# Sums of weight halves formed ahead and kept in DRAM, and an eighth seven-product square in six groups of a transformer block

## The chip, the cores and the metric

One core of one Trainium2 chip runs the whole kernel. The metric is the device time of one execution in microseconds (us). The kernel before took 2002.9 us, the median of three runs (2002.39 to 2003.01). A step called faster or slower here is one of more than 0.2%.

## The reference, cut to what matters

One layer of a block with two kinds of mixing: a chunked mLSTM with eight heads, and a sparse attention with sixteen heads in four groups. The width is 4096, the sequence 256 rows, everything in float32. Almost all of the arithmetic is in three large matrix products; the rest stands between them.

```python
h = _rmsnorm(x, norm_w[layer])
u = h @ w_in[layer]                       # 4096 x 13376: q, k, v and gates of both mixers
...
y_ml = hm.reshape(B, S, ML_WIDTH) * jax.nn.sigmoid(ml_o) * jax.nn.silu(ml_z)
y_ns = _nsa(ns_q, ...) * jax.nn.silu(ns_z)
x = x + jnp.concatenate([y_ml, y_ns], axis=-1) @ w_out[layer]
x = x + jax.nn.sigmoid(x @ ple_gate[layer]) * (p[layer] @ ple_proj[layer])
```

## The kernel before

**Units.** The weights are cut into units of 128 partitions x 1024 floats (512 KB), and the program is written out by hand as one list of them. SP loads a unit into one of six `raw` buffers (L1527 and the lines around it). ScalarE copies it to `whi`, rounded to the short float that TensorE multiplies in one pass (L1543). VectorE forms the rest, `wlo = raw - whi` (L1546). The activations are split the same way into `sh` and `sl`. TensorE adds up three products for each block, whi by sh, whi by sl and wlo by sh. There are four `whi` and four `wlo` buffers, and VectorE's subtraction is issued three units ahead of TensorE's use:

```python
for n in range(N):
    if n + LOOK < N:
        split_low(n + LOOK)        # VectorE, LOOK = 3
    ...
    load_some()                    # SP, while a raw buffer is free
    ...
    un["mm"](*splits.pop(n))       # TensorE
    ...
        split_high(n + 1 + LOOK)   # ScalarE
```

Loads are issued in the order of the units, each as soon as `held_raw` says that a buffer is free. All engines run their own instructions in order, so an instruction of another task that stands between two `wlo` subtractions on VectorE puts off the second of them.

**Stages.** First come the early pair groups and the "wide" groups (`wide_group`, TensorE lines L968 and L970). A wide unit has 12 matmuls. Beside the wide groups run the side tasks: the attention of the four head groups (L530 to L664), the convolutions of the mLSTM's q and k (L694, L696), the mLSTM itself, and the mixed activations (`t_mix`, L840 to L848). The wide groups that matter below are, in order, `nq2`, `nq3`, `mq0`, `mk0`, `mq1`, `mk1`, `mv2`, `mv3`. Then come the late pair groups, numbered -6 to 7 (`pair_group`, L1246): gates, the output projection and the last gate.

**Squares.** A pair group multiplies by 1024 columns at once, two halves whose results stand in the tiles `mm` and `sd`. Its 16 "squares" of 256 rows each are done in one of two ways. A square marked C takes the plain way: eight block products, 24 matmuls, two units. A mixed square takes seven block products in the manner of Strassen and Winograd, 21 matmuls. It has a part a (two units) and, after a C square that stands between, a part c (two units). Part c needs sums of the square's weight halves. VectorE forms them in place, in the two `raw` buffers that the square therefore holds until part c, by four dependent additions of 128 x 512 (L1327, L1329, L1331, L1332 in `sums`). Each follows a `wlo` subtraction of a later unit (`split_and_sum`). For the first unit of part a only one half is split (`split_one`, L1553 and L1556). A plan gives the order of the squares of a group; squares written in brackets share one C square between their parts.

```python
FULL = _plan((0,), (3, 5, 7, (9, 11), 13, 1), (2, 4, 6, 8, 10, 12), (14, 15))
PLANS = {g: FULL for g in (-5, -4, -3, -2, 1, 2)}
```

So each of these six groups has seven mixed squares and nine C squares.

## Time and profile before

| | |
|---|---|
| median of three runs | 2002.9 us |
| span of the profiled execution | 2001.0 us |
| what lies around the span in the median | 1.9 us |
| TensorE matmul (PE) busy | 1992.9 us, 9626 records |
| VectorE (DVE) busy | 1720.8 us |
| ScalarE (ACT) busy | 1210.8 us |
| GpSimd (POOL) busy | 23.3 us |
| DMA, mean over the span | 211 GB/s |

The shares are averages over stages with different limits, and matmuls overlap one another: the mean length of one matmul in the list of groups (379 to 389 ns) is longer than the distance from one to the next, which the chain of waits gives. Stretches of the program are named below by their time from the start of the span: the wide groups run from about 441 to 849 us, four of the six groups (-5 to -2) from about 934 to 1248 us and the other two (1 and 2) from 1415 to 1572 us.

### The profile page before, as it was taken

How to read it: one execution, taken by the hardware profiler on the slowest of the kernel's cores; microseconds unless marked ns; L12 is line 12 of the kernel's file. 1: busy time of each engine (PE TensorE's matmuls, PEld its weight loads, DVE VectorE, ACT ScalarE, POOL GpSimd, SP SyncE). 2: the span in 40 equal slices, each digit the busy share in tenths (PEclk: the TensorE clock that was granted, in tenths of full speed). 3: DMA queues.
4: the chain of work that ended last, by engine and by line, in shares of the span. 5: the costliest groups of instructions: out<-in, count | busy, mean ns of one | idle time of the engine just before them, and what ended most of it. 6: DMA issues, size and time to landing. Idle time of an engine off the chain costs nothing.

```text
span 2001.0 us, 26995 instructions
## 1 busy us (share of the span) xinstructions
PE 1992.9 (100%) x9626; PEld 1736.7 (87%) x9626; DVE 1720.8 (86%) x2235; ACT 1210.8 (61%) x1583; POOL 23.3 (1%) x59
## 2 busy tenths in 40 slices
PE   9999999999999999999999999999999999999998
PEld 8888888888888888888888888888888888888887
DVE  7797779787677776869999999999999998999988
ACT  7655556556666646566565666666555566666655
POOL 0000000000000000000000000000000000000000
PEclk9999999999999999999999999999999999999999
DMA  9656767575445455646666667565767674767664
GB/s 374 236 194 233 259 232 246 165 243 180 166 150 168 151 190 170 204 152 214 214 209 222 211 214 237 190 221 184 247 217 234 231 239 159 237 211 240 203 239 152
DMA packets 119351, 422.08 MB, mean 211 GB/s; under 512 B 14583, under 2 KB 14991, under 8 KB 119216
## 3 DMA queue, kind: packets, MB, share of 16 engines
q1 hardware_dynamic: 116880, 413.90, 61.2%
q0 software_dynamic: 2144, 6.44, 1.3%
q8 instruction: 75, 1.23, 0.2%
q14 instruction: 60, 0.49, 0.1%
q10 hardware_dynamic: 192, 0.02, 0.0%
HBM read 416.08 MB, written 4.23 MB: 210 GB/s over the span
## 4 chain that ended last, share of the span: by engine, by line
PE 98%; DVE 1%; DMA 0%; ACT 0%; issue 0%; SPq 0%; DVEq 0%; ACTq 0%
PE mm L1246 36%; PE sd L1246 34%; PE mm L968 14%; PE mm L970 7%; PE sd L639 1%; PE mm L1080 1%; PE sd L628 1%; PE sd L867 1%; PE sd L275 0%; DMA raw<-in_w_in 0%; PE sd L579 0%; PE sd L595 0%; PE sd L594 0%; PE sd L593 0%; PE mm L1056 0%; PE mm L1057 0%
## 5 line engine op out<-in xcount | busy, mean ns | idle before, releaser
L1543 ACT ACTIVATE whi<-raw 128x1024 fp32r<-128x1024 f32 x852 | 888.7, 1054 | 676.2 <-DVE raw L1332 155.1
L1546 DVE TENSOR_TENSOR wlo<-raw,whi 128x1024 fp32r<-128x1024 f32 x852 | 1035.3, 1221 | 186.4 <-ACT whi L1543 176.6
L1246 PE MATMUL mm<-whi,sh 128*128 128x512 f32 x897 | 281.6, 381 | 0.0
L1246 PE MATMUL mm<-wlo,sh 128*128 128x512 f32 x897 | 280.5, 380 | 0.0
L1246 PE MATMUL mm<-whi,sl 128*128 128x512 f32 x897 | 279.9, 379 | 0.0
L1246 PE MATMUL sd<-whi,sh 128*128 128x512 f32 x858 | 270.7, 380 | 0.0
L1246 PE MATMUL sd<-wlo,sh 128*128 128x512 f32 x858 | 270.3, 380 | 0.0
L1246 PE MATMUL sd<-whi,sl 128*128 128x512 f32 x858 | 269.7, 379 | 0.0
L968 PE MATMUL mm<-whi,sh 128*128 128x512 f32 x640 | 196.8, 389 | 0.2 <-ACT whi L1590 0.2
L1246 PEld LDWEIGHTS mm<-wlo,sh 128*128 128x128 f32 x897 | 169.0, 189 | 25.2 <-DVE wlo L1546 1.4
L1246 PEld LDWEIGHTS mm<-whi,sl 128*128 128x128 f32 x897 | 169.5, 189 | 24.1
L968 PE MATMUL mm<-whi,sl 128*128 128x512 f32 x640 | 190.4, 379 | 0.0
L970 PE MATMUL mm<-wlo,sh 128*128 128x512 f32 x640 | 190.3, 379 | 0.0
L1246 PEld LDWEIGHTS mm<-whi,sh 128*128 128x128 f32 x897 | 168.3, 189 | 23.6 <-issue 0.4
L1246 PEld LDWEIGHTS sd<-wlo,sh 128*128 128x128 f32 x858 | 161.7, 189 | 24.2 <-DVE wlo L1546 1.6
L1246 PEld LDWEIGHTS sd<-whi,sl 128*128 128x128 f32 x858 | 162.2, 189 | 23.0
L1246 PEld LDWEIGHTS sd<-whi,sh 128*128 128x128 f32 x858 | 161.3, 189 | 23.7 <-issue 0.4
L1246 PE MATMUL mm<-whi,cb 128*128 128x512 f32 x446 | 141.1, 379 | 0.0
L968 PEld LDWEIGHTS mm<-whi,sl 128*128 128x128 f32 x640 | 121.1, 189 | 17.3
L1246 PE MATMUL sd<-whi,cb 128*128 128x512 f32 x426 | 136.0, 379 | 0.0
L970 PEld LDWEIGHTS mm<-wlo,sh 128*128 128x128 f32 x640 | 121.0, 189 | 17.2
L968 PEld LDWEIGHTS mm<-whi,sh 128*128 128x128 f32 x640 | 116.0, 190 | 16.0 <-issue 1.6
(324 smaller groups left out, 1970.0 us busy)
## 6 DMA issues: line engine op xcount, KB each, us to landing
raw<-in_w_gate SPq DMA_DIRECT2D x192, 512.0 KB, 4.3
raw<-in_w_in SPq DMA_DIRECT2D x159, 512.0 KB, 3.9
raw<-in_w_early SPq DMA_DIRECT2D x128, 512.0 KB, 4.3
raw<-in_w_out SPq DMA_DIRECT2D x128, 512.0 KB, 4.4
raw<-in_ple_gate SPq DMA_DIRECT2D x128, 512.0 KB, 4.4
raw<-in_w SPq DMA_DIRECT2D x16, 512.0 KB, 5.5
u<-in_xt SPq DMA_DIRECT2D x16, 256.0 KB, 7.5
xn<-in_x SPq DMA_DIRECT2D x4, 1024.0 KB, 9.6
```

The source lines that it names most:

```text
L628: nc.tensor.transpose(psd[i][:, b, s, :], sb[i][:, b, s * 128:(s + 1) * 128], idn)
L639: MM(o[t][:, h, :], ptb[i][:, b, s, :], v[:, s, b, g * 128:(g + 1) * 128], start=False, stop=(i == 6 + t and b == 1 and s == t))
L867: nc.tensor.transpose(pp[i // 2][:, i % 2, t * 128:(t + 1) * 128], src[:, t, k:k + 128], idn)
L968: MM(box["ps"][t], s[c][:, k, t * 128:(t + 1) * 128], stream(m, j), start=st, stop=False)
L970: MM(box["ps"][t], sh[c][:, k, t * 128:(t + 1) * 128], stream(lo, j), start=False, stop=last)
L1080: MM(o[64 * kv:64 * kv + 60], xq[l // 8][:, l % 8, 60 * kv:60 * kv + 60], raw[:, j, 256 * kv:256 * kv + 256], start=l in (0, 24), stop=l i ...
L1246: MM(acc.t, s, m, start=acc.i == 0, stop=acc.i == acc.n - 1)
L1543: nc.scalar.activation(hi, r, AF.Copy)
L1546: nc.vector.tensor_sub(lo, r, hi)
```

## The change

Three things change. All six groups that had the plan FULL get the plan EIGHT, in which square 15 is mixed too (eight mixed squares, eight C squares). Its mixed activations are formed for the groups that multiply x (-6 to -1) and y (0 to 3); they stand in four small tiles of the tag `tb`. Second, for squares 7, 11 and 15 of the six groups (18 squares) the weight sums are no longer formed within the group. They are formed beforehand in 36 jobs, one for each half of a square, spread evenly over the units from the fifth of `nq2` to the twelfth before group -6, one in about three units. `begin_sums` loads 512 KB into a `raw` buffer on SP's queue. Three units later `end_sums` issues four dependent VectorE additions of 128 x 256 and a store of 512 KB to DRAM on GpSimd's queue. Third, a square with stored sums loads only the used half in the first unit of part a (256 KB) and doesn't hold its `raw` buffers; part c loads the two stored units from DRAM (512 KB each).

```diff
--- before.py
+++ after.py
@@ -69,7 +69,10 @@
 SIX = _plan((0, 1), MIXED, (2, 4, 6, 8, 10, 12), (14, 15))
 TWICE = (3, (5, 7), 9, 11, (13, 1))
 SHIFT = _plan((0,), TWICE, (2, 4, 6, 8, 10), (12, 14, 15))
-PLANS = {g: FULL for g in (-5, -4, -3, -2, 1, 2)}
+EXTRA = 15
+EIGHT = _plan((0,), (3, (5, 7), (9, 11), 13, (1, EXTRA)), (2, 4, 6, 8, 10), (12, 14))
+PLANS = {g: EIGHT for g in (-5, -4, -3, -2, 1, 2)}
+STASH = [(g, kp) for g in (-5, -4, -3, -2, 1, 2) for kp in (7, 11, EXTRA)]
...
@@ -807,7 +810,7 @@
                 held["cb"] = wk.tile([128, 2, 2, 4, 128], F32R, tag={3: "a", 7: "nat2", 11: "nat3"}[kp], name="cb")
             t = held["cb"][:, int(kp in (5, 9, 13))]
             return t[:, 0], t[:, 1]
-        if tag == "t":
+        if tag == "t" or kp == EXTRA:
             return [[wk.tile([128, 2, 128], F32R, tag="tb", name="cb", bufs=4) for _ in range(2)] for _ in range(2)]
         if kp == MORE:
             t = wk.tile([128, 2, 4, 128], F32R, tag="a" if tag == "b" else "b", name="cb")
...
@@ -871,7 +877,7 @@
             for half in range(2):
                 p, hs = pp[half], slice(2 * half, 2 * half + 2)
                 w = [hnw[:, col0 // 128 + 2 * half + i:col0 // 128 + 2 * half + i + 1] for i in range(2)] if scales else None
-                if 2 * c + half in MIXED or flag in (f"y{MORE // 2}", f"r{MORE // 2}") and half == MORE % 2:
+                if 2 * c + half in MIXED + (MORE,) * (flag[0] in "yr") + (EXTRA,) * (flag[0] == "y"):
                     f[half] = stile([128, 4, 128])
                     if scales:
                         for i in range(2):
@@ -1375,11 +1381,17 @@
             unit(w[kp, k], split, mm, kp, post=post)
 
         def a_units(kp):
+            ready = (g, kp) in stash
+
             def split1(r):
+                if ready:
+                    return split_one(r, False)
                 raw[kp] = [r]
                 return split_one(r)
 
             def split2(r):
+                if ready:
+                    return split_and_sum(r)
                 raw[kp].append(r)
                 low = split_all(r, keep=True)
 
@@ -1396,7 +1408,7 @@
             def mm2(hi, lo):
                 both(product(own[0][0], mixed(kp, 2), stream(hi, 0), stream(lo, 0)),
                      product(own[0][1], blocks(kp)(1, 0), stream(hi, 1), stream(lo, 1)))
-            unit(w[kp, 0], split1, mm1, kp, True)
+            unit(w[kp, 0][:, :, 256:512] if ready else w[kp, 0], split1, mm1, kp, True)
             unit(w[kp, 1], split2, mm2, kp, True)
 
         def c_units(kp, last):
@@ -1414,6 +1426,10 @@
                     urgent.append(t_x1_oth(g, oth) if 0 <= g < 4 else t_out_oth(g, oth, us))
                     if g in (-1, 3):
                         new_activations(g, range(2), 0)
+            if (g, kp) in stash:
+                for i, mm in enumerate((mm1, mm2)):
+                    unit(stash[g, kp][i], split_and_sum, mm, post=post if i else None)
+                return
             unit(None, lambda _: split_and_sum(raw[kp][0], kp), mm1)
             unit(None, lambda _: split_and_sum(raw[kp][1], kp), mm2, post=post)
 
@@ -1490,11 +1506,16 @@
             if g == 1:
                 add(t_p())
             if g == -6:
-                add(t_mix((MORE,), "x", "a", 3))
+                add(t_mix((MORE,), "x", "a", 3), t_mix((EXTRA,), "x", "a", 3))
         units[-1]["post"] = end
+
+    weights = {g: a["w_gate"][g + 6] if g < 0 else a["w_out"][g] if g < 4 else a["ple_gate"][g - 4] for g in range(-6, 8)}
+    stash = {key: drp.tile([2, 128, 2, 512], F32, name=f"sums{i}") for i, key in enumerate(STASH)}
+    begins = {}
 
     done.update(f"{n}{c}" for n in "ex" for c in range(8))
     for name in ORDER:
+        begins[name] = len(units)
         if name == "small":
             small_group()
         elif name in EARLY:
@@ -1503,12 +1524,9 @@
                 evq.extend(("oth-10", "oth-10"))
         else:
             wide_group(name, a["w_in"][WIDE.index(name)], None, p1_post(name))
-    for g in range(-6, 0):
-        pair_group(g, a["w_gate"][g + 6], "x")
-    for g in range(4):
-        pair_group(g, a["w_out"][g], "y")
-    for g in range(4, 8):
-        pair_group(g, a["ple_gate"][g - 4], "r")
+    begins[-6] = len(units)
+    for g, w in weights.items():
+        pair_group(g, w, "x" if g < 0 else "y" if g < 4 else "r")
 
 
     raws, splits = {}, {}
@@ -1524,7 +1542,8 @@
             for j in range(2):
                 nc.sync.dma_start(raws[n][:, j], units[n]["src"][:, j])
         else:
-            nc.sync.dma_start(raws[n], units[n]["src"])
+            src = units[n]["src"]
+            nc.sync.dma_start(cols(raws[n], 1) if src.shape[-1] == 256 else raws[n], src)
         if n in XN:
             j = XN.index(n)
             nat[j] = wk.tile([128, 2, 1024], F32, tag=f"nat{j}", name=f"xn{j}")
@@ -1548,12 +1567,13 @@
             return hi, lo
         return low
 
-    def split_one(r):
+    def split_one(r, keep=True):
         hi, lo = split_tiles()
         nc.scalar.activation(cols(hi, 0), cols(r, 1), AF.Copy)
 
         def low():
             nc.vector.tensor_sub(cols(lo, 0), cols(r, 1), cols(hi, 0))
+            held_raw[0] -= not keep
             return hi, lo
         return low
 
@@ -1608,6 +1628,31 @@
             held_raw[0] += 1
             load(loads.popleft())
 
+    jobs, begun = deque((key, h) for key in STASH for h in range(2)), deque()
+    when = deque(np.linspace(begins["nq2"] + 4, begins[-6] - 12, len(jobs)).astype(int).tolist())
+
+    def begin_sums(n):
+        if not (when and n >= when[0] and held_raw[0] < RAWB):
+            return
+        when.popleft()
+        held_raw[0] += 1
+        (g, kp), h = key = jobs.popleft()
+        r = wk.tile([128, 2, 512], F32, tag="raw", name="raw", bufs=RAWB)
+        nc.sync.dma_start(r, weights[g][kp, :, :, h].rearrange("k p c -> p k c"))
+        begun.append((n + 3, key, r))
+
+    def end_sums(n):
+        if begun and n >= begun[0][0]:
+            _, (key, h), r = begun.popleft()
+            add2 = nc.vector.tensor_add
+            b = [[r[:, k, 256 * j:256 * j + 256] for j in range(2)] for k in range(2)]
+            add2(b[0][1], b[0][1], b[0][0])
+            add2(b[0][0], b[0][0], b[1][0])
+            add2(b[1][0], b[1][0], b[0][1])
+            add2(b[1][1], b[1][1], b[1][0])
+            nc.gpsimd.dma_start(stash[key][:, :, h].rearrange("k p c -> p k c"), r)
+            held_raw[0] -= 1
+
...
@@ -1620,6 +1665,8 @@
             split_low(n + LOOK)
         while behind:
             behind.popleft()()
+        end_sums(n)
+        begin_sums(n)
         load_some()
         un = units[n]
         if un["pre"]:
```

How the change moves instructions is shown at three places. On VectorE, in the convolutions that run beside `mk1` and `mv2` (`wlo` is a unit's low part, `sq` and `u` belong to the convolution, `mv` is a result of a wide group), there stands before:

```order
L1546 TENSOR_TENSOR wlo<-raw,whi 128x1024
L220 TENSOR_SCALAR mv<-mm_6855,rt 128x2x256
L694 TENSOR_SCALAR sq<-u,convw_c 128x256
L696 SCALAR_TENSOR_TENSOR sq<-u,convw_c,sq 128x256 x3
L1546 TENSOR_TENSOR wlo<-raw,whi 128x1024 x3
L689 COPY u<-sd_7336 128x4x128
L1546 TENSOR_TENSOR wlo<-raw,whi 128x1024
```

and after (L1565, L223, L697, L699 and L692 are the same lines under new numbers):

```order
L1565 TENSOR_TENSOR wlo<-raw,whi 128x1024
L223 TENSOR_SCALAR mv<-mm_7076,rt 128x2x256
L697 TENSOR_SCALAR sq<-u,convw_c 128x256
L699 SCALAR_TENSOR_TENSOR sq<-u,convw_c,sq 128x256 x3
L1565 TENSOR_TENSOR wlo<-raw,whi 128x1024
L1649 TENSOR_TENSOR raw<-raw 128x256
L1650 TENSOR_TENSOR raw<-raw 128x256
L1651 TENSOR_TENSOR raw<-raw 128x256
L1652 TENSOR_TENSOR raw<-raw 128x256
L1565 TENSOR_TENSOR wlo<-raw,whi 128x1024 x2
L692 COPY u<-sd_7592 128x4x128
L1565 TENSOR_TENSOR wlo<-raw,whi 128x1024
```

Four additions of a job, L1649 to L1652, have come between two `wlo` of three that stood in a row. Numbering the `wlo` of this stretch from the first one after 790 us, the program after has a job behind the 1st, 4th, 7th, 10th and 14th.

On VectorE, in the second of the attention's head groups (`sc` holds the scores of the compressed keys, `s` those of the others), there stands before:

```order
L1546 TENSOR_TENSOR wlo<-raw,whi 128x1024
L550 TENSOR_TENSOR sc<-sd_4814,biasc 128x4x15 x2
L553 TENSOR_REDUCE mx_4841<-sc 128x8
L554 TENSOR_TENSOR sc<-sc,mx_4841 128x8x15
L604 TENSOR_TENSOR s<-sd_4846,tb 128x256
```

and after:

```order
L1565 TENSOR_TENSOR wlo<-raw,whi 128x1024
L1649 TENSOR_TENSOR raw<-raw 128x256
L1650 TENSOR_TENSOR raw<-raw 128x256
L1651 TENSOR_TENSOR raw<-raw 128x256
L1652 TENSOR_TENSOR raw<-raw 128x256
L553 TENSOR_TENSOR sc<-sd_4888,biasc 128x4x15 x2
L556 TENSOR_REDUCE mx_4922<-sc 128x8
L557 TENSOR_TENSOR sc<-sc,mx_4922 128x8x15
L607 TENSOR_TENSOR s<-sd_4927,tb 128x256
```

A job stands ahead of the scores (L550, now L553). It does so in the first three head groups; in the fourth a `wlo` still lies between the job and the scores.

On VectorE, in the parts of squares 9 and 11 of a late group, there stands before:

```order
L1546 TENSOR_TENSOR wlo<-raw,whi 128x1024
L1327 TENSOR_TENSOR raw<-raw 128x2x256
L1556 TENSOR_TENSOR wlo<-raw,whi 128x2x256
L1546 TENSOR_TENSOR wlo<-raw,whi 128x1024
L1327 TENSOR_TENSOR raw<-raw 128x2x256
L1546 TENSOR_TENSOR wlo<-raw,whi 128x1024
L1329 TENSOR_TENSOR raw<-raw 128x2x256
L1546 TENSOR_TENSOR wlo<-raw,whi 128x1024
L1331 TENSOR_TENSOR raw<-raw 128x2x256
L1332 TENSOR_TENSOR raw<-raw 128x2x256
```

and after:

```order
L1565 TENSOR_TENSOR wlo<-raw,whi 128x1024
L1333 TENSOR_TENSOR raw<-raw 128x2x256
L1575 TENSOR_TENSOR wlo<-raw,whi 128x2x256
L1565 TENSOR_TENSOR wlo<-raw,whi 128x1024
L1335 TENSOR_TENSOR raw<-raw 128x2x256
L1565 TENSOR_TENSOR wlo<-raw,whi 128x1024
L1337 TENSOR_TENSOR raw<-raw 128x2x256
L1338 TENSOR_TENSOR raw<-raw 128x2x256
L1565 TENSOR_TENSOR wlo<-raw,whi 128x1024 x5
```

L1333 to L1338 are the additions of `sums`, L1575 is that of `split_one`. One of the two squares' additions are gone, and five `wlo` follow one another.

## Rows read from the trace of the kernel before

**Rows 1.** The page's first part (busy time, share of the span, records of each engine) and the fourth (the chain of work that ended last, by engine).

```profile
PE 1992.9 (100%) x9626; PEld 1736.7 (87%) x9626; DVE 1720.8 (86%) x2235; ACT 1210.8 (61%) x1583; POOL 23.3 (1%) x59
...
PE 98%; DVE 1%; DMA 0%; ACT 0%; issue 0%; SPq 0%; DVEq 0%; ACTq 0%
```

**Rows 2.** The wait of TensorE's late matmuls in the list of waits over the whole span: engine, line, what was waited for, us in total, times, longest.

```profile
PE sd L1246 <- DVE wlo L1546: 0.2, 1, 0.2
```

**Rows 3.** The chain of work in order of time, pieces from the six groups: start, length in us, engine, output tile and line, number of matmuls.

```profile
984.01 6.58 PE sd L1246 x30
...
1013.25 5.18 PE mm L1246 x24
...
1019.08 6.47 PE mm L1246 x30
...
1542.84 6.58 PE mm L1246 x30
```

**Rows 4.** Groups of VectorE's instructions, forms apart: line, operation, tiles and shapes, count, then busy us and mean ns of one, then the idle time before them.

```profile
L1546 DVE TENSOR_TENSOR wlo<-raw,whi 128x1024 fp32r<-128x1024 f32 x852 | 1035.3, 1221 | 186.4 <-ACT whi L1543 176.6 <-PE sd L1246 0.2
...
L1556 DVE TENSOR_TENSOR wlo<-raw,whi 128x512 fp32r<-128x512 f32 x109 | 74.7, 685 | 8.0 <-ACT whi L1553 7.9
...
L1327 DVE TENSOR_TENSOR raw<-raw 128x512 f32<-128x512 f32 x109 | 74.6, 684 | 0.0
...
L842 DVE TENSOR_TENSOR s<-s 128x256 f32<-128x256 f32 x13 | 5.5, 425 | 0.5
```

**Rows 5.** Stretches of the span: start and end, length, then busy us and records of PE, PEld, DVE, ACT and POOL, then granted clock, busy share of the DMA engines and GB/s.

```profile
1013.00:1091.00 78.00, 78.00 (x363) 68.13 (x362) 73.95 (x85) 47.53 (x52) 0.00 (x0) 1.00 0.65 213
441.00:849.00 408.00, 408.00 (x2115) 358.52 (x2115) 292.94 (x494) 248.85 (x448) 12.12 (x28) 1.00 0.53 173
...
810.00:820.00 10.00, 10.00 (x48) 8.77 (x47) 9.79 (x15) 5.73 (x7) 0.00 (x0) 1.00 0.71 236
```

**Rows 6.** VectorE in order of time during the convolutions: start, length, line, operation, tiles, number of instructions, and in square brackets the idle time before and what ended it.

```profile
791.48 2.35 DVE L1546 TENSOR_TENSOR wlo<-raw,whi 128x1024 fp32r<-128x1024 f32 x2
...
809.77 3.49 DVE L1546 TENSOR_TENSOR wlo<-raw,whi 128x1024 fp32r<-128x1024 f32 x3
...
825.67 2.36 DVE L1546 TENSOR_TENSOR wlo<-raw,whi 128x1024 fp32r<-128x1024 f32 x2
...
828.67 0.42 DVE L842 TENSOR_TENSOR s<-s 128x256 f32<-128x256 f32 x1
829.13 0.29 DVE L843 TENSOR_TENSOR s<-s 128x128 f32<-128x128 f32 x1
```

**Rows 7.** TensorE in the same stretch, the first product with `wlo` of a unit, two times.

```profile
813.14 0.59 PE L970 MATMUL mm<-wlo,sh 128*128 128x512 f32 x2
...
833.86 0.59 PE L970 MATMUL mm<-wlo,sh 128*128 128x512 f32 x2
```

**Rows 8.** VectorE in order of time in the four head groups of the attention, columns as in rows 6.

```profile
479.90 0.42 DVE L604 TENSOR_TENSOR s<-sd,tb 128x256 f32<-128x256 f32 x1 [0.29 <-PE sd L595]
...
482.62 0.17 DVE L616 RECIPROCAL sm<-sm 128x2 f32<-128x2 f32 x1 [0.70 <-ACT s L611]
...
483.14 0.69 DVE L604 TENSOR_TENSOR s<-sd,tb 128x512 f32<-128x512 f32 x1 [0.17 <-PE sd L595]
...
485.54 0.35 DVE L568 TENSOR_TENSOR sc<-sc,mask_c 128x60 f32<-128x60 f32 x2
...
547.83 0.69 DVE L604 TENSOR_TENSOR s<-sd,tb 128x512 f32<-128x512 f32 x1 [0.56 <-PE sd L595]
...
550.22 0.35 DVE L568 TENSOR_TENSOR sc<-sc,mask_c 128x60 f32<-128x60 f32 x2
...
609.26 0.42 DVE L604 TENSOR_TENSOR s<-sd,tb 128x256 f32<-128x256 f32 x1 [0.30 <-PE sd L595]
...
612.50 0.69 DVE L604 TENSOR_TENSOR s<-sd,tb 128x512 f32<-128x512 f32 x1 [0.96 <-PE sd L595]
...
614.89 0.35 DVE L568 TENSOR_TENSOR sc<-sc,mask_c 128x60 f32<-128x60 f32 x2
...
666.26 1.23 DVE L1546 TENSOR_TENSOR wlo<-raw,whi 128x1024 fp32r<-128x1024 f32 x1 [1.32 <-ACT whi L1543]
```

**Rows 9.** TensorE in three of the same head groups, the transposes that take what VectorE's L568 wrote.

```profile
485.91 0.41 PE L574 MATMUL sd<-idn,sc 128*128 128x128 f32 x2
...
550.58 0.41 PE L574 MATMUL sd<-idn,sc 128*128 128x128 f32 x2
...
615.25 0.41 PE L574 MATMUL sd<-idn,sc 128*128 128x128 f32 x2
```

**Rows 10.** DMA issues: tiles, queue, count, KB each and median us from issue to landing.

```profile
raw<-in_w_gate SPq DMA_DIRECT2D x192, 512.0 KB, 4.3
raw<-in_w_in SPq DMA_DIRECT2D x159, 512.0 KB, 3.9
...
out_x<-u POOLq DMA_DIRECT2D x6, 512.0 KB, 4.6
```

**Rows 11.** The third part of the page, SP's queue: packets, MB, share of 16 engines' span.

```profile
q1 hardware_dynamic: 116880, 413.90, 61.2%
```

**Rows 12.** ScalarE in order of time where two squares share a C square, columns as in rows 6.

```profile
1047.17 2.00 ACT L1543 ACTIVATE whi<-raw 128x1024 fp32r<-128x1024 f32 x2 [0.67 <-PE mm L1246]
1049.38 1.06 ACT L1543 ACTIVATE whi<-raw 128x1024 fp32r<-128x1024 f32 x1 [0.21 <-DMA raw<-in_w_gate]
```

7 lines of the change are left out of this document (5 added, 2 removed).

## The prediction

> **What bounds the kernel now.** I read the page's first and fourth parts first. TensorE is busy for 1992.9 of 2001.0 us, and 98% of the chain that ended last is TensorE's, 1% VectorE's [rows 1]. So a change is worth what it takes from TensorE's own work, less what it makes TensorE wait. The list of waits has next to nothing for the late groups, one wait of 0.2 us for `wlo` [rows 2], but that list shows only single waits that the profile can name. The chain in order of time shows the smaller ones: a run of 24 matmuls lasts 5.18 us, 215.8 ns each, and one of 30 lasts 6.47 us, the same pace; in seven pieces of 30 in the six groups (the first and the last stand in the rows) it lasts about 6.58 [rows 3]. The matmuls' mean lengths in the list of groups are not used, since matmuls overlap.
>
> Then I asked where VectorE has room, since the change moves work on it. In group -4 it is busy for 73.95 of 78 us. Over the whole wide phase it is busy for 292.94 of 408 us, so on the average there is room for more. But that is an average over unlike stretches: during the convolutions it is busy for 9.79 of 10 us [rows 5].
>
> **The change, part by part.**
>
> *Fewer matmuls.* Six squares go from 24 to 21 matmuls: 18 x 215.8 ns = 3.9 us less on TensorE, all on the path. The program's order confirms 18 fewer TensorE rows.
>
> The Trainium skill, "TensorE: Matmul & The Clock Gate", section "Back-to-back issue gap", gives about 131 ns for each matmul of 512 columns in a sustained stream with its weight load, and about 216 ns only for an isolated one. By it the 18 would save 2.4 us and the sum below would end at 2004.7. The trace disagrees: this is a sustained stream, and it runs at 215.8 ns.
>
> *VectorE in the six groups.* Additions of 128 x 512 take 0.684 us, a `wlo` of a whole unit 1.22, of half a unit 0.685 [rows 4]. Each group had 7 squares with 4 additions and now has 5 (3, 5, 9, 13, 1): 8 x 0.685 = 5.5 us less. Square 15 as a mixed one has 3 whole and one half `wlo` for 2 whole ones: 1.22 + 0.685 = 1.9 more. Net 3.6 us less of 73.95 in a group, against TensorE's 0.65 less. The seven late pieces cost 7 x 0.11 = 0.8 us; I take them as gone, with 0 as the other end. The new mixed activations of square 15 are five VectorE steps, about 2.4 us each for x and for y (two of 128 x 512 at 0.685, one of 128 x 256 at 0.42, two of 128 x 128 at 0.29 [rows 4, 6]); the room just won covers the first, group 0, whose plan has only four mixed squares, the second. Cost nothing; without this cover at most 2 x 2.4.
>
> *What a job costs VectorE.* No row shows four additions of 128 x 256 in a chain. One lasts 0.425 us [rows 4]; a step that uses it begins 829.13 - 828.67 = 0.46 later [rows 6]. Independent ones overlap by about 0.085 (three `wlo` of 1.22 take 3.49 us), so the last frees the engine after 0.34. A job is 3 x 0.46 + 0.34 = 1.72 us; bounds 4 x 0.34 = 1.36 and 4 x 0.46 = 1.84. All 36 are 62 us on top of 293 in the 408 us. Where VectorE has idle time they cost nothing. Two places have none.
>
> *The convolutions, 790 to 834 us.* VectorE works nearly without a break there, and its lead over TensorE is small. Number the `wlo` from the first of the pair at 791.48. The 7th is the first of the three at 809.77 and ends at 810.99; counting the units on both engines, TensorE uses it at 813.14, a lead of 2.15 us. The 15th is the second of the pair at 825.67 and ends at 828.03; it is used at 833.86 (eight units of 12 matmuls later), a lead of 5.83 [rows 6, 7]. The new order puts jobs behind the 1st, 4th, 7th, 10th and 14th. Two stand ahead of the 7th: 2.15 - 3.44 = -1.3. Five stand ahead of the 15th: 5.83 - 8.6 = -2.8. A wait of TensorE's moves all later uses, so these are not added; the largest counts: +2.8 us. With the bounds of a job 5 x 1.36 - 5.83 = 1.0 to 5 x 1.84 - 5.83 = 3.4; nothing if VectorE has a lead that my count misses. Behind a job wait the next `wlo`, the convolution's step and the copies out of PSUM, all for the same 1.72 us.
>
> *The attention.* In a head group TensorE's side work waits directly for VectorE: L568 starts at 485.54, 550.22 and 614.89, lasts 0.35, and the transposes L574 begin at 485.91, 550.58 and 615.25, within 0.02 us of its end [rows 8, 9]. All of TensorE's stream stands behind them. Between a job's new place, ahead of the scores, and L568, VectorE has idle times that take up part of the 1.72 us. First group: 0.29 + 0.70 + 0.17 = 1.16, leaves 0.56. Second: 0.56, leaves 1.16. Third: 0.30 + 0.96 = 1.26, leaves 0.46. In the fourth the job comes ahead of a `wlo` before which VectorE is idle for 1.32 us [rows 8], and the rest goes in a later idle time: 0. Together +2.2 us. The lower end is 0 (the idle times hide everything, or the transposes could start earlier than the rows show); the upper one 4 x 1.84 = 7.4, if no idle time helps.
>
> *Loads and stores.* A unit of 512 KB costs 61.2% x 2001 us / 413.9 MB = 1.55 us of all 16 DMA engines [rows 11]. 36 loads and, priced the same, 36 stores add 112 us to a busy share of 0.53 of 408 us [rows 5]: about 0.80. A load lands in 3.9 us there; a store on GpSimd's queue I price by `out_x`, 4.6 us [rows 10], so a buffer is held for 6.3 us from the first addition on. What is queued behind it is SP's loads, issued in order: a load into that buffer waits for the store to land. Six buffers of 2.6 us of TensorE each (12 x 215.8 ns) are 15.5 us of stock and cover that; cost nothing, and if the cover failed in all 36 jobs by half a microsecond each, 18 us. GpSimd, busy for 23.3 us in all, has room for 36 issues. In the late groups a load more or less is covered as long as TensorE's three units of stock last (see the second rival).
>
> *The sum*, against the profiled execution: 2001.0 - 3.9 - 0.8 + 2.8 + 2.2 = 2001.3 us, and with the 1.9 us that the median has around the span **2003.2 us**. The gain and the new waits are of one size. A measurement of this kernel can tell about 0.2% (4 us) from no change, so this counts as the same.
>
> **Rivals.**
>
> *The jobs are hidden.* VectorE's idle times and its lead take up all of them, in the convolutions too. For it: 115 us of idle time in the wide phase, and no wait of TensorE for VectorE there now. Against it: in the two places the lead is smaller than the jobs that come ahead, by rows. Time: 2002.9 - 3.9 - 0.8 = 1998.2 us. If only one of the two places is hidden, 2000.4 or 2001.0, still the same by the bound above.
>
> *Late loads in the six groups (slower).* Where two mixed squares share a C square, 66 matmuls (14.24 us) used to come with 6 loads, 9.3 us of the DMA engines; with one of the two stored it is 7.5 loads, 11.6 us, 82%. At such a place ScalarE had already waited 0.21 us for a load [rows 12]. One more load ahead makes it 0.21 + 1.55 = 1.76 us late. It decides once this lateness goes through ScalarE and VectorE to TensorE, that is, once the stock of three units is used up. At one place in each of six groups that is between 0 and 10.6 us; the middle, 5.3, gives 2008.5 us. Against it: the stored squares hold no `raw` buffers between their parts, so loads can be issued earlier than now, and VectorE has 3.6 us more room in each group to catch up.
>
> *The attention's idle times don't help (slower).* 36 jobs fall on other side steps as well; with the upper end, 7.4 for 2.2, the time is 2008.4 us. The rows of idle time speak against it.
>
> **How the numbers follow.** Sum as worked out, with its smaller mixtures: 0.57. Hidden: 0.22. Late loads: 0.12. Attention at its upper end: 0.09. The forecast is that of the first, 2003.2 us. The lower end of the range is the hidden case, 1998.2; the upper end takes in the two slower cases at their prices and a little for what lies beyond the middle of the second: 2009.0. Faster by over 0.2% means below 1998.9, which the hidden case alone gives: 0.22. Slower means above 2006.9, the last two: 0.21. The same: 0.57.
>
> **What would show it right or wrong.** TensorE 18 matmuls shorter, and no piece of 6.58 us in the six groups. New waits of TensorE for `wlo` near 810 to 834 us, about 2.8 us together. L574, the transposes, later against the units around them in the first three head groups by 0.6, 1.2 and 0.5 us. A job of 1.72 us between its first addition and the next instruction. If TensorE has no gap in the wide phase, the first rival is right; if ScalarE waits for loads in the six groups and TensorE then waits for `wlo`, the second. I would be wrong altogether if TensorE waited at a place not named here, such as the step from the wide groups to group -6, or for the stored sums.

## The result, and the profile after

The changed kernel took 2017.0 us, the median of four runs (2015.3 to 2018.2), against 2002.6 us for the kernel before in the same comparison: a ratio of 1.0070, 95% interval 1.0057 to 1.0082. The forecast was 2003.2 us, between 1998.2 and 2009.0. The change makes the kernel slower, and the time lies outside the range.

The span of the profiled execution is 2014.6 us, 13.6 more than before. The page's first part and its chain stand first; they answer to [rows 1].

```profile
PE 1993.6 (99%) x9608; PEld 1735.1 (86%) x9608; DVE 1761.1 (87%) x2353; ACT 1226.1 (61%) x1600; POOL 49.6 (2%) x95
...
PE 92%; DVE 5%; issue 1%; ACT 1%; DMA 1%; SPq 0%; DVEq 0%; ACTq 0%
```

TensorE has 18 matmuls less, as counted, but its share of the chain fell from 98% to 92%, and VectorE's rose from 1% to 5%. The list of TensorE's waits was nearly empty before [rows 2]. Now it reads (engine, line, what was waited for, us in total, times, longest):

```profile
PE sd L596 <- DVE s L607: 2.9, 3, 1.4
PE sd L742 <- ACT mqk L703: 2.4, 1, 2.4
PE sd L1252 <- DVE wlo L1565: 1.8, 3, 1.4
PE sd L577 <- DVE sc L571: 1.7, 2, 1.1
...
PE sd L766 <- DVE pt L761: 1.2, 1, 1.2
...
PE mm L976 <- DVE wlo L1565: 0.9, 2, 0.6
```

Only the last line and L577 (L574 before) are waits that the prediction had named. L596 is the attention's score products, L742 and L766 belong to the mLSTM, L1252 to a late group. The list shows only waits of some length; the offsets below have the small ones too.

In the wide phase TensorE's program is the same before and after, so its instructions can be paired one by one, and the growth of the offset between the two traces tells where time was lost. Offsets by stage, from both traces (times of the kernel before):

```
stage                                 us lost   forecast
441 to 700   attention                  +7.2      +2.2
700 to 790   first convolutions, mLSTM  +5.9       0
790 to 836   last convolutions          +2.8      +2.8
836 to 932   mLSTM's end, group -6       0.0       0
behind 932   the other late groups      -2.3      -4.7
```

The sum is +13.6 us, where 2.2 + 2.8 - 4.7 = +0.3 was forecast. Four places show how it came about, one for each line with a loss and one for the missing gain.

**Attention.** VectorE and then TensorE in order of time in the first head group (start, length, line, operation, tiles, count, idle time before and its releaser):

```profile
492.38 0.16 DVE L620 TENSOR_TENSOR sm<-sm,sg 128x2 f32<-128x2 f32 x1
492.46 0.43 DVE L1649 TENSOR_TENSOR raw<-raw 128x256 f32<-128x256 f32 x1
492.92 0.43 DVE L1650 TENSOR_TENSOR raw<-raw 128x256 f32<-128x256 f32 x1
493.38 0.43 DVE L1651 TENSOR_TENSOR raw<-raw 128x256 f32<-128x256 f32 x1
493.84 0.42 DVE L1652 TENSOR_TENSOR raw<-raw 128x256 f32<-128x256 f32 x1
494.18 0.68 DVE L607 TENSOR_TENSOR s<-sd,tb 128x512 f32<-128x512 f32 x1
```

```profile
494.92 0.38 PE L596 MATMUL sd<-kh,qh 128*128 128x256 f32 x1 [1.37 <-DVE s L607]
```

A job lasts 494.18 - 492.46 = 1.72 us, the predicted price. Behind it stands L607, which empties the PSUM tile that the next score product L596 writes. TensorE waits until L607 has ended, and its whole stream waits with it. Before, the same step ended 0.25 us ahead of the product:

```profile
491.28 0.68 DVE L604 TENSOR_TENSOR s<-sd,tb 128x512 f32<-128x512 f32 x1
```

```profile
492.21 0.27 PE L593 MATMUL sd<-kh,qh 128*128 128x256 f32 x1
```

So the lead is 0.25 us, the job takes 1.72, and 1.5 are lost. By the pairing, L596 cost 4.1 us in all, most of it behind jobs at 492.46, 559.26 and 685.63, and L534, which waits for a copy (L517) behind another job, 0.9. Their leads before were 0.3 to 1.0 us. No term stood for these two. L577 cost 1.2, 0.8, 0.3 and 0 us in the four head groups, 2.2 in all. The sum is that of the prediction; the parts are not (0.6, 1.2, 0.5 and 0 were forecast). In the first group one idle time did not take up what was counted on:

```profile
484.06 0.17 DVE L619 RECIPROCAL sm<-sm 128x2 f32<-128x2 f32 x1 [0.85 <-ACT s L614]
```

It was 0.70 us before [rows 8] and is 0.85 now. It ends with steps of ScalarE's (L561, then L614) that themselves wait for VectorE's scores, so it moved along with the job and absorbed nothing.

**First convolutions and mLSTM.** VectorE, ScalarE and TensorE there:

```profile
742.70 0.42 DVE L1649 TENSOR_TENSOR raw<-raw 128x256 f32<-128x256 f32 x1 [2.00 <-DMA raw<-in_w_out]
...
753.30 0.42 DVE L1649 TENSOR_TENSOR raw<-raw 128x256 f32<-128x256 f32 x1
...
755.40 1.52 DVE L699 SCALAR_TENSOR_TENSOR sq<-u,convw_c,sq 128x256 f32<-128x256 f32 x3
```

```profile
751.14 1.06 ACT L1562 ACTIVATE whi<-raw 128x1024 fp32r<-128x1024 f32 x1 [2.62 <-DMA raw<-in_w_in]
756.96 1.06 ACT L703 ACTIVATE mqk<-sq 128x1024 f32<-128x1024 f32 x1 [4.76 <-DVE sq L699]
```

```profile
758.07 0.70 PE L742 MATMUL sd<-mqk 128*128 128x256 f32 x2 [2.44 <-ACT mqk L703]
...
760.96 1.06 PE L974 MATMUL mm<-whi,sh 128*128 128x512 f32 x2
...
763.10 0.59 PE L974 MATMUL mm<-whi,sh 128*128 128x512 f32 x2
```

Two jobs stand in the chain from the convolution (`sq`) to `mqk` to L742. One of them also held VectorE idle for 2.00 us, because its own load had not landed; ScalarE was idle for 2.62 us until a weight load landed. TensorE waited 2.44 us. Before, `mqk` was ready 3.4 us ahead of its use:

```profile
743.87 1.04 ACT L700 ACTIVATE mqk<-sq 128x1024 f32<-128x1024 f32 x1
```

```profile
748.32 0.59 PE L739 MATMUL sd<-mqk 128*128 128x256 f32 x2
```

The two jobs (3.44 us) just use up this lead, and the 2.00 us go beyond it. Then eight matmuls ran at half the pace: they start 0.43 us apart in place of 0.216, and a pair lasts 1.06 us in place of 0.59. The windows over the same time (length, busy PE, PEld, DVE, ACT, POOL, granted clock, DMA share, GB/s) show the granted clock at 0.87 and 0.56:

```profile
757.00:760.00 3.00, 1.93 (x8) 1.74 (x9) 3.00 (x3) 2.91 (x3) 0.22 (x1) 0.87 0.78 201
760.00:763.00 3.00, 3.00 (x9) 2.35 (x9) 2.90 (x6) 0.00 (x0) 0.67 (x1) 0.56 0.80 279
```

So these 5.9 us are 2.7 for L742, 1.7 for the slow matmuls (eight times 0.21) and 1.5 for L766. Ahead of L766 stand another job, at 770.61, and two `wlo` for which VectorE was idle 2.72 and 1.35 us, since ScalarE had waited 5.24 us for a weight load. L766 had a lead of 2.5 us before, so the job alone would not have reached it.

**Last convolutions.** 2.8 us, in short waits for `wlo` between 820 and 850 us, as predicted by place and size. The longest:

```profile
820.93 0.70 PE L976 MATMUL mm<-wlo,sh 128*128 128x512 f32 x2 [0.63 <-DVE wlo L1565]
```

**Group -5.** VectorE where TensorE waited longest in the late groups, and that wait:

```profile
966.84 0.68 DVE L839 TENSOR_TENSOR cb<-s,cb 128x512 fp32r<-128x512 f32 x1
967.44 0.69 DVE L845 TENSOR_TENSOR s<-sh,sl 128x512 f32<-128x512 f32 x1
968.16 0.43 DVE L847 TENSOR_TENSOR s<-s 128x256 f32<-128x256 f32 x1
...
969.16 1.22 DVE L1565 TENSOR_TENSOR wlo<-raw,whi 128x1024 fp32r<-128x1024 f32 x1
```

```profile
970.43 0.48 PE L1252 MATMUL sd<-wlo,cb 128*128 128x512 f32 x1 [1.40 <-DVE wlo L1565]
```

Two sets of mixed activations (`cb`, `s`) follow one another ahead of a `wlo`. TensorE loses 2.1 us at this place (two shorter waits behind it included), by the distances between its matmuls. The six groups' own pieces of 6.58 us [rows 3] are gone in all but two places, and VectorE has the room that was forecast for it (compare [rows 5]):

```profile
1026.50:1104.00 77.50, 77.50 (x361) 67.94 (x360) 70.80 (x77) 49.58 (x54) 0.00 (x0) 1.00 0.74 246
```

### The profile page after: what moved, and what is told of

Same layout as the page of the kernel before. It is cut to its first block, busy times and chain, and to the rows that moved or that the text cites. A ratio compares the mean times of both kernels' runs of the same rounds, so it can differ in the third digit from the quotient of the medians.

```text
span 2014.6 us, 27308 instructions
## 1 busy us (share of the span) xinstructions
PE 1993.6 (99%) x9608; PEld 1735.1 (86%) x9608; DVE 1761.1 (87%) x2353; ACT 1226.1 (61%) x1600; POOL 49.6 (2%) x95
## 4 chain that ended last, share of the span: by engine, by line
PE 92%; DVE 5%; issue 1%; ACT 1%; DMA 1%; SPq 0%; DVEq 0%; ACTq 0%
PE mm L1252 35%; PE sd L1252 34%; PE mm L974 11%; PE mm L976 5%; DVE wlo L1565 2%; PE sd L642 1%; DVE sq L699 1%; PE mm L1086 1%; PE sd L873 1%; PE sd L631 0%; ACT whi L1562 0%; PE sd L278 0%; DVE s L607 0%; PE sd L582 0%; DMA raw<-in_w_in 0%
## 5 line engine op out<-in xcount | busy, mean ns | idle before, releaser
L1565 DVE TENSOR_TENSOR wlo<-raw,whi 128x1024 fp32r<-128x1024 f32 x858 | 1039.1, 1221 | 170.1 <-ACT whi L1562 159.2
L1252 PE MATMUL mm<-whi,sh 128*128 128x512 f32 x882 | 278.0, 381 | 0.0
L1252 PE MATMUL mm<-wlo,sh 128*128 128x512 f32 x882 | 276.6, 380 | 0.2 <-DVE wlo L1565 0.2
L1252 PE MATMUL mm<-whi,sl 128*128 128x512 f32 x882 | 276.3, 379 | 0.0
L1252 PE MATMUL sd<-whi,sh 128*128 128x512 f32 x843 | 267.1, 380 | 0.0
L1252 PE MATMUL sd<-wlo,sh 128*128 128x512 f32 x843 | 266.6, 380 | 0.2 <-DVE wlo L1565 0.2
L1252 PE MATMUL sd<-whi,sl 128*128 128x512 f32 x843 | 266.1, 379 | 0.0
L1252 PEld LDWEIGHTS mm<-wlo,sh 128*128 128x128 f32 x882 | 166.6, 189 | 24.3 <-DVE wlo L1565 1.0
L1252 PEld LDWEIGHTS mm<-whi,sl 128*128 128x128 f32 x882 | 166.9, 189 | 23.5
L1252 PEld LDWEIGHTS mm<-whi,sh 128*128 128x128 f32 x882 | 165.7, 189 | 23.0 <-ACT whi L1572 0.4
L1252 PEld LDWEIGHTS sd<-wlo,sh 128*128 128x128 f32 x843 | 159.1, 189 | 24.1 <-DVE wlo L1565 1.8
L1252 PEld LDWEIGHTS sd<-whi,sl 128*128 128x128 f32 x843 | 159.5, 189 | 22.4
L1252 PEld LDWEIGHTS sd<-whi,sh 128*128 128x128 f32 x843 | 158.7, 189 | 23.1 <-ACT sq L354 0.4
L1252 PE MATMUL mm<-whi,cb 128*128 128x512 f32 x470 | 148.8, 379 | 0.0
L1252 PE MATMUL sd<-whi,cb 128*128 128x512 f32 x450 | 143.7, 379 | 0.0
```

Of the source, the lines that this page charges most:

```text
L1252: MM(acc.t, s, m, start=acc.i == 0, stop=acc.i == acc.n - 1)
L1565: nc.vector.tensor_sub(lo, r, hi)
```

## The experiments

Two theories were set against each other: V, that VectorE's additions stand ahead of small steps for which TensorE waits, and T, that the jobs' loads and stores make the weight loads late. Diffs are against the changed kernel unless another is named. Where "lost" is said of a stage, it is the growth of the offset to the kernel before, found as above in the one profiled run. In the first 20 us, where no job runs, single traces already differ by -0.7 to +1.8 us from the kernel before; that is part of the times, but not of the losses by stage.

**Additions left out.**

```diff
-            add2(b[0][1], b[0][1], b[0][0])
-            add2(b[0][0], b[0][0], b[1][0])
-            add2(b[1][0], b[1][0], b[0][1])
-            add2(b[1][1], b[1][1], b[1][0])
```

> The 36 jobs keep their loads and stores but leave out the four VectorE additions (the stored units are the plain weights, so the squares 7, 11 and 15 of the six groups are not computed as they should be). The changed kernel lost 15.9 us in the wide phase and won 2.3 us behind it. Theory V (VectorE's additions stand ahead of small steps that TensorE waits for): the wide phase loses under 1 us, total 2000 to 2002 us. Rival T (the loads and stores of the jobs make the weight loads late): the loss stays, 2012 us or more.

2004.6 us, ten runs between 2000.7 and 2010.9; ratio 1.001 (1.0000 to 1.0019). In the profiled run the offset does not change by 0.02 us from 441 to 836 us, with all loads and stores in place, although SP's weight loads waited 135.2 us for stores in that run, for 72.0 in the changed kernel. Without the additions nothing is lost up to there. The exception is one place at the end, 2.0 us. GpSimd, SP, ScalarE and TensorE there:

```profile
832.11 0.71 POOL L1647 DMA_DIRECT2D sums<-raw  x1 [11.71 <-DVE s L849]
```

```profile
825.63 10.60 SPq L1546 DMA_DIRECT2D raw<-in_w_in  x3
836.34 12.77 SPq L1546 DMA_DIRECT2D raw<-in_w_gate  x8
```

```profile
842.48 1.06 ACT L1562 ACTIVATE whi<-raw 128x1024 fp32r<-128x1024 f32 x1 [6.97 <-DMA raw<-in_w_in]
```

```profile
849.37 0.67 PE L766 MATMUL sd<-mv,pt 128*128 128x257 f32 x2 [1.75 <-DVE pt L761]
```

SP issues loads in order, and one of three took until 836 us to go out, since its buffer was still being stored. ScalarE then waited 6.97 us for a weight load. What TensorE missed was not the `wlo`, which has a lead, but L761, a small step queued on VectorE behind the late `wlo`. The wide spread of the runs may mean that such places come and go from run to run; only one of the ten was traced.

**Stores left out.**

```diff
-            nc.gpsimd.dma_start(stash[key][:, :, h].rearrange("k p c -> p k c"), r)
...
-                    unit(stash[g, kp][i], split_and_sum, mm, post=post if i else None)
+                    unit(w[kp, i], split_and_sum, mm, post=post if i else None)
```

> The jobs load and add, but the 36 stores are left out, and part c loads plain weights in place of the stored sums (same bytes; the squares 7, 11 and 15 of the six groups are not computed as they should be). A raw buffer comes free right behind the additions. Theory V: nearly the whole loss stays, 2012 to 2016 us (the one wait of 2.0 us for a job's own load near the mLSTM may go). Rival T: without stores the loads are in time, 2000 to 2004 us.

2013.2 us, ratio 1.0055 (1.0038 to 1.0071). Attention 7.1 us and last convolutions 2.8, as in the changed kernel; first convolutions and mLSTM 1.9 in place of 5.9. So V holds for 11.9 of 15.9 us, and 4.0 us hang on the stores as well, all at one place: without them the job's own load holds VectorE up for 1.18 us in place of 2.00, L742 waits 1.6 us, no matmul runs at half pace behind it, and L766 does not wait.

```profile
758.24 0.70 PE L742 MATMUL sd<-mqk 128*128 128x256 f32 x2 [1.62 <-ACT mqk L703]
```

**Additions on GpSimd.**

```diff
-            add2 = nc.vector.tensor_add
+            add2 = nc.gpsimd.tensor_add
```

> The same four additions on GpSimd, which is busy for 50 of 2015 us, ahead of the store on its own queue; all is computed. Theory V: VectorE's order is that of before in the wide phase, so its loss goes: 2000 to 2002 us. Rival T: transfers are the same, 2012 us or more. A third possibility: the additions on GpSimd are so slow, or so much in VectorE's way, that buffers are held for longer and the loss comes back as late loads.

2118.3 us, ratio 1.0575 (1.0559 to 1.0591). The third possibility, far beyond what was expected. SP's wait for stores, ScalarE's for loads, and one of the four additions:

```profile
SPq L1546 <- DMA sums<-raw: 346.1, 29, 14.8
```

```profile
ACT whi L1562 <- DMA raw<-in_w_in: 200.8, 51, 9.9
```

```profile
L1649 POOL TENSOR_TENSOR raw<-raw 128x256 f32<-128x256 f32 x36 | 38.7, 1076 | 449.7 <-DMA raw<-in_w_gate 256.6 <-DMA raw<-in_w_out 74.0 <-DMA raw<-in_w_in 31.5
```

An addition takes 1.08 us on GpSimd for 0.42 on VectorE, and there is other work in GpSimd's queue. Each buffer is held for longer, SP's in-order loads stand behind it, and the loss is for the most part T's mechanism in the open: SP's weight loads wait 346 us for stores, for 72 in the changed kernel, and ScalarE 200.8 us for loads, for 16.5.

**No jobs at all.**

```diff
-        if not (when and n >= when[0] and held_raw[0] < RAWB):
-            return
+        return
```

> No jobs at all: neither loads, additions nor stores in the wide phase, and part c loads plain weights (same bytes; the squares 7, 11 and 15 of the six groups are not computed as they should be). It shows the late groups alone. Both theories: the wide phase as before, within 0.2 us; total 2002.9 - 2.3 = 2000.6 us, with about 2 us of waits of TensorE for VectorE in group -5 near the mixed activations of square 15.

2001.3 us, ratio 0.9991 (0.9982 to 1.0001); nothing lost in the wide phase, and the late groups 2.1 us shorter in the profiled run. The time is 0.7 us above the expected one, the two stages are as expected.

**One addition per unit.**

```diff
-            _, (key, h), r = begun.popleft()
+            at, (key, h), r = job[:3]
...
+            nc.vector.tensor_add(d, d, e)
+            job[3] += 1
+            if job[3] == 4:
```

> Each job's four additions are issued one per unit over four units in place of all at once; loads, stores and the total work on VectorE are the same, and all is computed. Theory V: what hurts is the 1.72 us by which a job puts off the small step behind it; now that is 0.46 us, which the idle times of 0.3 to 1.3 us near the attention mostly take up: the attention's 7.1 us fall to about 2, the mLSTM's 5.9 to about 2.5, the convolutions' 2.8 stay, since VectorE has no idle time there at all: about 2008 us. Rival W (it is the amount of work on VectorE in these stretches that counts, not how it is cut): 2015 us or more.

2014.7 us, ratio 1.0058 (1.0040 to 1.0077). The attention fell from 7.2 to 3.5 us with the same work on VectorE, the direction of V and against W, though W's number (2015 us or more) is nearly met; last convolutions 2.5. But first convolutions and mLSTM lost 4.9, and 5.3 came at a new place behind 836. There GpSimd's queue is the cause:

```profile
850.73 0.71 POOL L1655 DMA_DIRECT2D sums<-raw  x1 [10.45 <-DVE raw L1651]
851.43 2.17 POOL L731 DMA_DIRECT2D mb<-mrow_d  x4
```

```profile
858.60 0.42 DVE L751 TENSOR_TENSOR s<-mb,future_c 128x256 f32<-128x256 f32 x1 [5.29 <-DMA mb<-mrow_d]
```

The loads of `mb` for the mLSTM stand behind a store, and the store behind the additions. Jobs that last for four units keep their buffers and GpSimd's queue for longer. The price of V went down and another went up.

**Jobs earlier.**

```diff
-    when = deque(np.linspace(begins["nq2"] + 4, begins[-6] - 12, len(jobs)).astype(int).tolist())
+    when = deque(np.linspace(begins["nq2"] - 20, begins["nq2"] + 84, len(jobs)).astype(int).tolist())
```

> The 36 jobs are whole again but spread from 20 units before nq2 to 84 units behind its start, so that none falls on the last convolutions or beside the mLSTM; all is computed. Theory V: the 2.8 us of the convolutions and the 5.9 us around the mLSTM go, the attention's 7.1 stay or grow to 8, since jobs are closer: 2008 to 2010 us, and TensorE's offset against before stops growing at about 700 us. Rival T (transfers): the same bytes in less time, so the loss stays at 14 us or grows.

2023.9 us, ratio 1.0106 (1.0091 to 1.0121). The offset stops growing at 700 us, as V says: nothing is lost beside the mLSTM and the convolutions. But 9.5 us went before 441 us, in the early pair group, whose mixed squares hold `raw` buffers and fill VectorE themselves (49.94 of 56 us before, from 385 to 441 us), and 13.2 from 441 to 700. In that stage VectorE once stood 2.30 us in front of a job whose own load had not landed, and L534 behind it waited 4.5 us. That price had been left out.

**Mixed activations of square 15 in group -6** (against the kernel without jobs).

```diff
-                add(t_mix((MORE,), "x", "a", 3), t_mix((EXTRA,), "x", "a", 3))
+                add(t_mix((MORE,), "x", "a", 3))
...
-                    add(t_mix((13,), "x", "a", 1), t_mix((3, 5), "x", "a", 2))
+                    add(t_mix((13,), "x", "a", 1), t_mix((3, 5), "x", "a", 2), t_mix((EXTRA,), "x", "a", 2))
```

> As e4_no_jobs (no jobs, part c loads plain weights, so the squares 7, 11 and 15 of the six groups are not computed as they should be), but the mixed activations of square 15 for x are formed in group -6, behind those of 3 and 5, and no longer in group -5. Theory: the 2 us that TensorE waited for VectorE in group -5 (near 970 us in the changed kernel) are these five VectorE steps; they go, 1999.3 us. Rival: those waits come from group -5's own squares, and the time stays at 2001.3 us.

2000.6 us, ratio 0.9988 (0.9979 to 0.9998), where 1999.3 was expected. The waits near 955 us fell from 2.1 to 0.4 us, so the theory of their cause holds; but a new one of 1.3 us stands in group -6. The steps had not found a place without a price. This run also bounds the change: with jobs that cost nothing, and the steps where they stand here, it would win 0.12%.

**The three edits together** (one addition per unit, jobs earlier, mixed activations in group -6).

> Additions one per unit, jobs from 20 units before nq2 to 84 behind its start, and the mixed activations of square 15 in group -6; all is computed. Theory V: -3.9 and up to -0.8 us in the late groups, 1 to 3 us lost in the attention: 1999 to 2002 us. Rival T: 2008 us or more.

2022.5 us, ratio 1.0098 (1.0083 to 1.0113); V's number was wrong for the same reason as that of the jobs placed earlier: 10.1 us before 441 and 7.8 more until 478. From 500 to 836 only 2.5 us were lost. Group -6 lost 1.4 us, and behind 932 it won 4.2.

**Buffers given back later** (the first against the kernel with one addition per unit, the second against the changed kernel).

```diff
-                held_raw[0] -= 1
+                stored.append(n + 2)
...
+        while stored and n >= stored[0]:
+            stored.popleft()
+            held_raw[0] -= 1
```

> As e5_single_adds (one addition per unit), but a job's raw buffer counts as free only two units after its store is issued, so that SP gives a weight load a buffer of another unit and not one whose store is still under way; all is computed. In e5 SP's loads waited 94 us for the stores, and TensorE lost 15 us in the wide phase, a part of it where ScalarE waited for loads. Theory V + T (both the additions' place and the buffers held by stores cost): SP's wait for stores falls below 30 us, the waits behind late loads go, and 4 to 7 us stay (the additions in the attention and the convolutions' 2.8): 2005 to 2008 us. Rival: the stock of buffers is what counts, and a buffer out of use for longer makes loads later still: 2014 us or more.

> The changed kernel with whole jobs, and the same later release of the buffer as in e9; all is computed. The run without stores lost 12 us in the wide phase, the changed kernel 15.9, so theory V + T gives about 12 us in the wide phase and 2012 to 2014 us. If the stores' buffers were nothing but a bystander: 2016 to 2017 us. If the loads become late for want of buffers: over 2018 us.

2015.8 us (ratio 1.0063, 1.0046 to 1.0080) and 2015.4 us (1.0062, 1.0047 to 1.0077). SP's wait for stores hardly changed. That of the weight loads rose, from 93.7 to 118.7 us and from 72.0 to 95.8, and that of the jobs' own loads fell, from 39.7 to 8.5 us and from 19.7 to nothing; together 127.2 us for 133.4, and 95.8 for 91.7. In the first the rival is right: a buffer out of use for longer is no help. The second lies between its first two numbers. Its wide phase lost 13.4 us for 15.9, 2.5 less, and nearly all of that between 700 and 790 us. With as much waiting on SP and less loss, the sum of SP's waits is no measure of the price; what counts is which small step stands behind the late unit, as the run without additions showed already.

**24 jobs** (squares 11 and 15 stored, then 7 and 15; against the kernel with one addition per unit and late release, with the mixed activations in group -6).

```diff
-STASH = [(g, kp) for g in (-5, -4, -3, -2, 1, 2) for kp in (7, 11, EXTRA)]
+STASH = [(g, kp) for g in (-5, -4, -3, -2, 1, 2) for kp in (11, EXTRA)]
...
-    when = deque(np.linspace(begins["nq2"] + 4, begins[-6] - 12, len(jobs)).astype(int).tolist())
+    when = deque(np.linspace(begins["nq2"] + 4, begins["nq2"] + 84, len(jobs)).astype(int).tolist())
```

> As e9, with sums stored for squares 11 and 15 only (24 jobs, those of square 7 are formed in the group again), the jobs between the fifth unit of nq2 and 84 units behind its start, and the mixed activations of square 15 in group -6; all is computed. Theory V + T: fewer jobs, none on the last convolutions or beside the mLSTM: 1 to 3 us lost in the attention; late groups -3.9, with up to 1 us of waits where 5 and 7 share a C square: 2000 to 2003 us. Rival: the density of jobs doesn't matter and the loss stays at 10 us: 2010 us.

> As e11_24_jobs, but the stored squares are 7 and 15, so that it is squares 9 and 11 that both form their sums in the group, as in the kernel before; and the mixed activations in group -6 follow one another faster. All is computed. Theory (a group's first shared C square comes before VectorE has a lead; the second one, as before, costs 0.1 us a group): late groups -3.9, wide phase +0.9 as in e11, up to 0.8 us left in groups -6 and -5: about 2000.5 us. Rival: any two unstored squares that share a C square cost what e11 showed (0.3 to 0.5 us a group): 2004 to 2005 us.

2005.3 us (ratio 1.0013, 1.0004 to 1.0022) and 2006.2 us (1.0016, 1.0007 to 1.0025). In both the wide phase until 836 us lost only 1.0 us: few jobs, cut into single additions and clear of the places without idle time, are nearly free. The rest gave it back. Group -6 lost 1.4 us in the first, to the mixed activations, and 2.5 in the second, where they follow one another faster. As to the late groups, behind 932 the first is 0.7 us longer than before and the second 0.1, where the run with the same steps in group -6 and no jobs is 3.9 shorter. So a pair that shares a C square and forms both sums in the group makes TensorE wait, 5 and 7 as well as 9 and 11, by 0.7 to 0.8 us a group; the rival of the second run is right in kind, and its price was too low. The first run met neither of its numbers.

**No stored sums.**

```diff
-STASH = [(g, kp) for g in (-5, -4, -3, -2, 1, 2) for kp in (7, 11, EXTRA)]
+STASH = [(g, kp) for g in (-5, -4, -3, -2, 1, 2) for kp in ()]
```

> The eighth square without any stored sums: no jobs, all sums formed in the group; all is computed. By the terms of the prediction VectorE then has 73.95 + 1.9 + 2.7 = 78.6 us of work in a group of 77.35 us of TensorE: at least 1.25 us of waits in each of six groups, 7.5 us in all, against -3.9 us: 2006.5 us or more. Rival (VectorE's lead from the C squares at both ends of a group covers it): 2001 us.

2012.6 us, ratio 1.0048 (1.0034 to 1.0062). A group of 79 us, and the waits for `wlo`:

```profile
1004.00:1083.00 79.00, 78.45 (x360) 67.09 (x359) 77.55 (x91) 48.81 (x54) 0.00 (x0) 1.00 0.66 211
```

```profile
PE sd L1252 <- DVE wlo L1565: 3.8, 10, 1.4
PE mm L1252 <- DVE wlo L1565: 2.2, 8, 0.4
```

VectorE is busy for 77.55 of 79.00 us, and the late groups are 10.4 us longer than before. So the stored sums do what they are for: they are worth 10.4 + 2.3 = 12.7 us behind 932. They cost 15.9 ahead of it. The theory is right, and its lower bound of 2006.5 us holds.

**36 jobs in a shorter stretch** (as the second run with 24 jobs).

```diff
-STASH = [(g, kp) for g in (-5, -4, -3, -2, 1, 2) for kp in (7, EXTRA)]
+STASH = [(g, kp) for g in (-5, -4, -3, -2, 1, 2) for kp in (7, 11, EXTRA)]
```

> As e12, but with all 36 jobs (squares 7, 11 and 15 stored) in the same stretch, from the fifth unit of nq2 to 84 behind its start; all is computed. Theory V + T: 0.44 jobs per unit in place of 0.3; the idle times near the attention take up less, and more buffers are out of use: 2 to 5 us lost in the wide phase, late groups -4.7: 2000 to 2003 us. Rival (loss grows with the bytes only): about 1.4 us in the wide phase, 1999.6 us.

2032.1 us, ratio 1.0154 (1.0138 to 1.0170); the profiled run is the slowest of its four, 2040.0. Its waits:

```profile
PE sd L596 <- DVE s L607: 11.3, 5, 3.9
```

```profile
ACT whi L1562 <- DMA raw<-in_w_in: 65.5, 33, 7.0
```

Half as many jobs again in the same 80 units cost 36 us in the wide phase of this run for 1.0; the median is 8 us below this run, so it loses some 28 there, as an estimate. No theory had that. A job of this form keeps its buffer for about eight units, so 36 keep 36 x 8 / 80 = 3.6 of the six out of use on the average and 24 keep 2.4. ScalarE waited 65.5 us for loads, for 7.1 with 24 jobs. How much of the 36 us comes from the buffers and how much from the denser additions was not separated.

## Why the prediction was wrong

The sum for the profiled execution was 2001.3 us, and it took 2014.6. Of the 13.3 us, 5.0 are the attention, 5.9 the first convolutions and the mLSTM, and 2.4 the late groups, nearly all in group -5.

**TensorE's saving: right.** 18 matmuls less, at the pace of before.

**VectorE in the six groups: right for the groups, wrong for the mixed activations.** 70.8 us of work in a group for 73.95 (3.2 less; 3.6 were forecast), and the waits of about 0.1 us are nearly gone. The step that failed is "the room just won covers the first": room on the average of a group doesn't help where two sets of five steps meet the place at which VectorE is behind. It cost 2.1 us, the end "at most 2 x 2.4" of the prediction being 2.4 for it. The kernel without jobs shows it alone, and forming these steps in group -6 moved most of it there.

**The price of a job: right.** 1.72 us, measured.

**The last convolutions: right**, 2.8 us. Counting the lead of `wlo` over TensorE and taking the jobs from it gave place and size.

**The attention: the mechanism was right and the term too small.** "In a head group TensorE's side work waits directly for VectorE" is what happens. The 2.2 us worked out for L568 and L574 (now L571 and L577) are what these lost, but that the sum fits to a tenth is luck: the three parts miss by up to 0.6 us, and an idle time of 0.70 us that was subtracted did not help. The larger error is that I followed one small step and one job in each head group and priced them as if they were the attention. Further jobs stand ahead of the scores (L607 for L596) and of L517 (for L534), whose leads of 0.3 to 1.0 us are less than a job, and these lost 5.0 us more. The kernel without additions lost nothing there, so all 7.2 are the additions'. The third rival, attention at its upper end, is near in number, 7.4 us, and it did say that jobs fall on other side steps; its sum of four whole jobs is not what happened.

**The mLSTM: no term.** "Where VectorE has idle time they cost nothing. Two places have none" is the step that failed: VectorE has idle time between 740 and 790 us, and I did not ask what stands behind a job there. The chain from the convolution through `mqk` to L742 crosses three engines with a lead of 3.4 us, two jobs and the wait for one job's load take 5.4, and L766 with a lead of 2.5 us was reached by a job and late loads together. Counting the lead as in the last convolutions would have shown that two jobs use all of it; the wait for a job's own load had no term at all. The place cost 5.9 us, of which 4.0 go when the stores go.

**Loads and stores: "cost nothing" was wrong in this one place.** The stock of TensorE's units did cover the late loads, as I argued. But VectorE works in order, and a `wlo` or a job that waits for its load keeps the small steps behind it waiting too. The stock covers the weights and not these steps. The second rival sought late loads in the six groups; there they did no harm that the runs show.

No clock term stood in the prediction either: of the 5.9 us, 1.7 are the half pace behind a wait.

No version run here beats the kernel before by more than the 0.12% of the run without the jobs' cost, which computes something else. Among those that compute everything, the best took 2005.3 us.

## What to carry to other kernels

An engine's idle share says how much work fits in, not where: ask of every place where work is put in which instruction stands next in that engine's queue, and how much lead it has over the engine that waits for it. Weight preparation with a lead of several units absorbs a microsecond or two; a small step absorbs only its own lead (here 0.02 to 1.0 us in the attention, 2.5 and 3.4 us in the mLSTM), and a delay of any cause (an addition, a late load, a store ahead in a queue) reaches it through the in-order queue. An idle time absorbs a delay only if what ends it doesn't itself wait for the delayed engine. Price all such steps of a stage, not the one that was looked at first; and a buffer that must be stored before it is free belongs in the account of every engine that issues into it in order.

## What the runs showed of the hardware that was not expected

Behind a long wait TensorE can run at half pace for a while. The traces with GpSimd's additions and with 36 jobs in the shorter stretch, whose waits crowd, are left out of this count. In the others there are eleven places where 2.5 to 4.9 us lie between two matmuls; behind seven of them 3 to 12 matmuls start 0.43 us apart in place of 0.216, which costs 0.6 to 2.5 us. Of some thirty places with 1.2 to 2.2 us only one shows it, for a single matmul, and that is the second of three waits within 12 us. The slow matmuls begin 3.2 to 4.1 us (once 6.5) behind the last matmul ahead of the wait, in six of the seven places after TensorE has started again. The run with 36 jobs in the shorter stretch shows that the length of a wait does not decide it: behind 3.14 us at 563 us seven matmuls are slow, behind 3.08 us at 627 us none. The Trainium skill, "TensorE: Matmul & The Clock Gate", section "What's actually happening", gives an idle window of about 3.4 us, free-running, as the condition and half the clock as the effect. The half pace agrees with it, and so does the chance in where it strikes; but 2.8 us between two matmuls, at 758 us of the changed kernel, were enough, so 3.4 us is no safe bound for a wait.

GpSimd's additions of 128 x 256 took 0.72 us in some places and up to 1.7 in others of the same run, 1.08 on the average for L1649. The Trainium skill, "GPSIMD Engine Reference", section "Specifications", says that its interface to SBUF is shared with VectorE, which contends with it in instructions with two SBUF inputs. The trace agrees. Of the 144 additions 52 took more than 0.8 us, and 50 of these run beside a `wlo` subtraction, whose two inputs are in SBUF; of the 92 shorter ones 16 do. VectorE pays as well: from 441 to 960 us 47 of its whole `wlo` run beside an addition and take 1.35 us on the average, and up to 1.80, for 1.22 of the others.
